# Oldest free page first, stores planned later on the queue, and down groups of 3, 4 and 4 pairs

## The chip, the cores and the metric

The kernel runs as one program on one core of a Trainium2 chip. The metric is the device time of one execution in microseconds (us): 2784.7 us as the median of three runs (2784.27 to 2785.05). The engines are named as the profile names them: PE (TensorE, matmuls), PEld (its weight loads), DVE (VectorE), ACT (ScalarE), POOL (GpSimd) and SP, whose queue issues every DMA of this kernel.

## The reference, cut to what matters

One layer is computed for a prompt of 2048 tokens of width 1024 and for a sample of 32 tokens with a cache of 512. In float32:

```python
mod = einsum(silu(c), w_ada) + b_ada                      # six vectors: shift, scale, gate, twice
h   = rms_norm(x, g_norm1) * (1 + scale1) + shift1
z   = einsum('bld,de->ble', h, w_in)                      # qa ka va | qr kr vr gr
oa  = diff_attention(qa, ka, va, ...)                     # 4 heads, two softmax maps each
orr = rms_unit(retention(rotate(qr), rotate(kr), vr)) * silu(gr)   # 4 heads, a running state
x   = x + gate1 * einsum(concat(oa, orr), w_out)
h2  = rms_norm(x, g_norm2) * (1 + scale2) + shift2
ff  = silu(einsum(h2, w_ff_gate)) * einsum(h2, w_ff_up)   # 2816 columns
x   = x + gate2 * einsum(ff, w_ff_down)
```

Besides both outputs x it returns the normed keys, the values and the last retention state (`k_prompt`, `v_prompt`, `ret_prompt`, and the same for the sample).

## The kernel before, in words

**Stages.** The prompt's 2048 tokens are 16 tiles of 128, in 4 groups of 4. *Start*: the modulation vectors are computed from 16 blocks `wa` of `w_ada`, tiles 0 to 3 of x are normed, and the first input weights are split into two float32r parts (`whi`, `wlo`), which are also stored to `w_scrA`/`w_scrR` and loaded from there by later groups. *Mixer*: for each group, four attention jobs (A0 to A3) and four retention jobs (R0 to R3); a job projects four tiles with three matmuls per product (high x high, high x low, low x high), then does its head. Keys go to `k_prompt` (from tile `qk`), values to `v_prompt` and `v_scr`, transposed keys to `kT_scr`, heads' outputs to `o_scr`. *wout*: the output projection. *gu0* and *gu1*: gate and up projections of the FFN for each half of the tokens. *down0* to *down2*: the down projection.

**Seven products.** From wout on, matrices are multiplied by `quad`: two tiles of rows at a time, as 2x2 blocks with seven products instead of eight. One side is *resident* for the stage (`res`: seven pieces per pair of 128-row blocks), the other is *streamed* (`str`: seven pieces per quad). A piece is a sum of blocks made by DVE, rounded by ACT, and the remainder subtracted by DVE. The down projection has 11 pairs of blocks, which `GROUPS` splits into groups; each group is a stage of 8 quads. A quad of nk pairs is 7 x 3 x nk matmuls of 512 columns: 84 for four pairs, 63 for three. A stage after the first adds the partial y of the stage before from `y_scr`; the last one also multiplies by gate2, adds x (`x2_scr`) and stores `y_prompt`.

**What sets the order.** The code only records operations (`_Plan.add`). `_Plan.schedule` then plays the program through with a cost for each operation (`_cost`, `PACE`) and a latency between engines (`LAT`): each engine takes, of the operations that are ready, the one recorded first (`rank`), if there is room for the tiles that it writes. The order in which an engine took its operations in this play is the order in which they are issued. SP takes DMAs in that order too, and a DMA that has to wait holds all behind it. An operation is ready when the last of its predecessors has ended in the play, plus the latency (`s.at`).

**Pages.** Tiles live in pages of 128 x 1024 floats of SBUF: 27 of kind R (float32r), 16 of kind F, and 7 that are F until the mixer's end and R after it (*swing*); PSUM is 8 banks. `_Places.take` gives a tile the page with the lowest number of those that are free, of the smallest size that fits. A tag's `bufs` bounds how many of its tiles live at once.

Of the kernel before, what the change touches and what calls it, by code (L numbers as in the profile page):

```python
# [12 lines left out]
F32 = mybir.dt.float32  # L13
# [7 lines left out]
P = 128  # L21
# [3 lines left out]
NT = SEQ // P  # L25
# [6 lines left out]
GT = 4  # L32
NG = NT // GT
NEG = -1e30
NR, NFP, NX = 27, 16, 7
GROUPS = ((0, 4), (8, 4), (16, 3))
LAM_INIT = 0.8 - 0.6 * math.exp(-0.3 * 0)
GAMMA = [1.0 - 2.0 ** (-5 - h) for h in range(NH)]


class _Op:
    __slots__ = ("engines", "call", "cost", "preds", "succs", "prio", "rank", "pos", "news", "uses", "left", "at")


class _Engine:
# [12 lines left out]
class _Tile:  # L58


    __slots__ = ("name", "space", "size", "cap", "acc", "old", "order", "block", "left", "dead", "kind", "brief")
# [8 lines left out]
class _View:  # L70


    __slots__ = ("tile", "p0", "np", "off", "dims", "dtype")
# [108 lines left out]
class _Places:  # L182


    def __init__(self, pages, rows, smallest):
        self.rows, self.smallest = rows, smallest
        self.sizes = sorted({rows[i] for i in pages})
        self.free, self.left = {}, 0
        for i in pages:
            self._add(i)  # L190

    def _add(self, i):
        self.free.setdefault(self.rows[i], set()).add((i, 0))
        self.left += 1

# [9 lines left out]
    def take(self, n, keep, but=()):  # L205
        size = self._size(n)
        best = None
        for s in sorted(self.free):
            if s >= size:
                fit = [b for b in self.free[s] if b[0] not in but]  # L210
                if fit:
                    best, (i, off) = s, min(fit)
                    break
        if best is None:
            return None
        whole = best == self.rows[i]
        if whole and self.left <= keep:
            return None
        self.free[best].discard((i, off))
        if whole:  # L220
            self.left -= 1
            if size != best and best > 1024:
                best = 1024
        while best > size:
            best //= 2
            self.free.setdefault(best, set()).add((i, off + best))
        return i, off, size
# [26 lines left out]
class _Plan:  # L254
# [105 lines left out]
    def add(self, engines, name, args, kw):  # L360
        op = _Op()
        op.prio = len(self.ops)
        op.rank = (op.prio + self.bias, op.prio)
        op.engines = engines
        op.call = (name, args, kw)
        op.cost = {e: self._cost(e, name, args, kw) * self.PACE.get(e, 1.0) for e in engines}
        op.preds, op.succs, op.news, op.uses = set(), [], [], set()
        writes = [args[0]] + ([kw["accum_out"]] if kw.get("accum_out") is not None else [])
        reads = list(args[1:]) + [v for k, v in kw.items() if k != "accum_out"]
        for x in reads:  # L370
            r = self._region(x)
            if r is None:
                continue
            t = r[0]
            for o, w, m, a, b in t.acc:
                if w and m & r[1] and a < r[3] and r[2] < b:
                    op.preds.add(o)
            t.acc.append((op, False, *r[1:]))
            op.uses.add(t)
        for x in writes:  # L380
            r = self._region(x)
            if r is None:
                continue
            t = r[0]
            fresh = True
            for o, w, m, a, b in t.acc:
                if m & r[1] and a < r[3] and r[2] < b and o is not op:
                    op.preds.add(o)
                    fresh = False
            if t.old is not None and fresh:  # L390
                self.firsts.append((op, t.old))
            if t.cap is not None:
                op.news.append(t)
            t.acc.append((op, True, *r[1:]))
            op.uses.add(t)
        op.preds.discard(op)
        self.ops.append(op)
        return op
# [15 lines left out]
    def schedule(self, places, swing):  # L414
# [3 lines left out]
        pos = 0.0  # L418
        order = {k: [] for k in places}
        for op in ops:  # L420
            op.pos = pos
            pos += op.cost.get("pe", 0.0)
            op.left = len(op.preds)
            op.at = 0.0
            for p in op.preds:
                p.succs.append(op)
            op.uses = [t for t in op.uses if t.cap is not None]
            for t in op.uses:
                t.left += 1
            for t in op.news:  # L430
                if t.order is None:
                    if t.space == "sb":
                        if any(v.dtype == F32R for o in t.acc for v in self._args(o[0], t)):
                            t.kind = "R"
                    t.brief = max(o[0].prio for o in t.acc) < self.cut
                    t.order = len(order[t.kind])
                    order[t.kind].append(t)
# [41 lines left out]
        while len(started) < len(ops):  # L479
            for e in sorted(idle):  # L480
                skipped, q = [], ready[e]
                while q:
                    pr, op = heapq.heappop(q)
                    if op in started:
                        continue
                    if not room(op):
                        skipped.append((pr, op))
                        continue
                    started[op] = (now, e)
                    idle.discard(e)  # L490
                    end = now + op.cost[e]
                    if e == "pe":
                        turn = op.call[0] == "transpose" and op.call[1][0].dtype == F32R
                        end += 54 * (turned and not turn)
                        turned = turn
                    push(end, 0, e)
                    for s in op.succs:
                        s.at = max(s.at, end + max(self.LAT[e][x] for x in s.engines))
                        s.left -= 1
                        if not s.left:  # L500
                            push(s.at, 1, s)
                    for t in op.uses:
                        t.left -= 1
                        lat = self.LAT[e]["pe"] if t.space == "ps" else max(self.LAT[e].values())
                        t.dead = max(t.dead, end + lat)
                        if not t.left:
                            push(t.dead, 2, t)
                    if op is ops[front]:
                        while front < len(ops) and ops[front] in started:
                            front += 1  # L510
                        while beyond and front < len(ops) and beyond[0][1].pos <= ops[front].pos + self.AHEAD:
                            _, o = heapq.heappop(beyond)
                            for x in o.engines:
                                heapq.heappush(ready[x], (o.rank, o))
                    break
                for x in skipped:
                    heapq.heappush(q, x)
# [67 lines left out]
def kernel(  # L585
# [12 lines left out]
    PE, ANY, AG = _Engine(plan, ["pe"]), _Engine(plan, ["act", "dve"]), _Engine(plan, ["act", "pool"])  # L598
    VG = _Engine(plan, ["dve", "pool"])
    dma = _Engine(plan, ["dma"]).dma_start  # L600

    def open_pool(stack, name, bufs, space=bass.MemoryType.SB):
        pool = stack.enter_context(tc.tile_pool(name=name, bufs=bufs, space=space, reuse_waits="tile"))
# [100 lines left out]
    if True:  # L704
# [99 lines left out]
        def prep_w(out, kind, h, first, sample):  # L804
# [4 lines left out]
            for kp in range(4):  # L809
# [6 lines left out]
                if first:  # L816
                    split(hi, lo, raw)
                    for x, d in zip((hi, lo), kept):
                        dma(d.bitcast(F32), x.bitcast(F32))
                else:  # L820
                    for x, d in zip((hi, lo), kept):
                        dma(x.bitcast(F32), d.bitcast(F32))
# [118 lines left out]
        def attn_back(h, t, vs, g, pt, inv):  # L941
# [8 lines left out]
                    last_u.append(PE.matmul(u[:, :P], lhsT=at[:, b * P:(b + 1) * P], rhs=vs[gv][:, bv, :],  # L950
                                            start=(gg == 0 and b == 0), stop=(gg == g and b == len(blocks) - 1)))
            o = head_out(u[:, :P], inv[:, 0:1], f"{h}_{t}")
            dma(o_scr[t][:, h * P:(h + 1) * P], o)

        def attn_front(h, t, z, kTs, vs):
            g, lt = divmod(t, GT)
            V_t = vs[g]
            A.copy(V_t[:, lt, :], z[:, 256:384])
            qk = qk_norm(z[:, 0:256], f"{h}_{t}")
            dma(k_prompt[t * P:(t + 1) * P, h * P:(h + 1) * P], qk[:, 2:4, :].rearrange("p a b -> p (a b)"))  # L960
            qs = wk.tile([P, 4, 2, 64], F32R, tag="qs", name=f"qs{h}_{t}", bufs=2)
            qh = qs[:, 0:2]
            qd = qk[:, 0:2, None, :].broadcast_to([P, 2, 2, 64])
# [67 lines left out]
        def ret_back(h, t, vr, sg, rk, rT):  # L1031
# [14 lines left out]
            PE.matmul(ra[:, 128:256], lhsT=sc, rhs=vr, start=(S is None), stop=True)  # L1046
            S_cur[h] = S2
            o = ret_out(ra[:, 128:256], sg, name)
            dma(o_scr[t][:, 512 + h * P:512 + (h + 1) * P], o)
            if t == NT - 1:  # L1050
                dma(ret_prompt[h], S2)

# [246 lines left out]
        for n, (g, kind, h) in enumerate(jobs):  # L1299
# [26 lines left out]
            for t in range(g * GT, (g + 1) * GT):  # L1326
# [4 lines left out]
                if kind == "A":  # L1331
                    qT, kb = attn_front(h, t, z, kTs, vs)
                    if t % GT == GT - 1:
                        dma(v_prompt[NG * h + g], vs[g].rearrange("p t c -> p (t c)"))
                        if g < NG - 1:
                            dma(kT_scr[h][g].bitcast(F32), kTs[g].bitcast(F32))
                            dma(v_scr[h][g], vs[g])
                    flush()
                    st_ = attn_mid(h, t, qT, kb, kTs)
                    pend.append(lambda h=h, t=t, vs=vs, st_=st_: attn_back(h, t, vs, *st_))  # L1340
# [475 lines left out]
```

## Time and profile before

| | us |
|---|---|
| median of three runs | 2784.7 |
| the profiled execution | 2783.05 |
| its span, first to last instruction | 2781.3 |
| PE busy | 2685.2 |
| PEld busy | 2229.1 |
| DVE busy | 1896.2 |
| ACT busy | 1307.1 |
| POOL busy | 249.3 |

The mean granted clock of TensorE is 0.984 of 2.4 GHz. PE is idle for 2781.3 - 2685.2 = 96.1 us of the span. Nearly every operation is issued by one line (L580 in the kernel before, L583 after), so groups of instructions are told apart by tiles and by time. In tile names `sb` is a page of SBUF, `ps` a bank of PSUM, `swing` a swing page. `SPq` rows are DMAs being issued: a DMA's row starts when its waits are over, or includes the waits of a merged run of DMAs (x2 and more).

### The profile page before, as it was taken

Reading aid. Unit: us, or ns where it says so; the run is one execution under the profiler, and the core shown is the slowest. Engines: PE = TensorE matmul, PEld = TensorE weight load, DVE = VectorE, ACT = ScalarE, POOL = GpSimd, SP = SyncE. Lnnn points to the kernel's source line nnn. Section 1 sums busy time; section 2 is a strip of 40 time slices with the busy share of each in tenths; the row PEclk is TensorE's granted clock in tenths of the full one; section 3 lists DMA queues with packets and bytes.
Section 4 is the critical chain, followed back from the end, with each engine's and each line's share of the span. In section 5 each row is a group of like instructions: output and inputs, shape, how many; then the busy total and the mean of one; then the engine's idle time right before and its main releaser. Section 6 shows DMA issues by size and latency. Waiting matters only on the chain.

```text
span 2781.3 us, 42347 instructions
## 1 busy us (share of the span) xinstructions
PE 2685.2 (97%) x14606; PEld 2229.1 (80%) x14606; DVE 1896.2 (68%) x4378; ACT 1307.1 (47%) x3241; POOL 249.3 (9%) x474
## 2 busy tenths in 40 slices
PE   6999999999999999989989999998999999999997
PEld 4889888889988888867868888886888887888875
DVE  3776656666676766696785565667655668577799
ACT  4556544666677755555573333243333324242331
POOL 0222111211111111131000000000000000000000
PEclk9999999999999999989999999999999999999999
DMA  7778666644555455546562222324333333355466
GB/s 265 256 270 280 211 207 226 204 153 158 164 170 168 150 189 154 183 139 205 177 202 69 83 61 85 106 83 145 106 99 107 114 121 121 130 180 175 165 229 223
DMA packets 309383, 454.16 MB, mean 163 GB/s; under 512 B 23752, under 2 KB 205196, under 8 KB 309168
## 3 DMA queue, kind: packets, MB, share of 16 engines
q1 hardware_dynamic: 309168, 451.46, 49.6%
q8 instruction: 115, 1.88, 0.3%
q14 instruction: 100, 0.82, 0.1%
HBM read 329.44 MB, written 121.40 MB: 162 GB/s over the span
## 4 chain that ended last, share of the span: by engine, by line
PE 88%; DVE 5%; DMA 3%; ACT 2%; issue 2%; SPq 0%; POOL 0%; DVEq 0%; ACTq 0%; POOLq 0%
PE ps L580 88%; DVE sb L580 4%; ACT sb L580 1%; DMA sb<-in_w_ada 1%; DMA sb<-in_w_ff_down 1%; DMA sb<-w_scrA 0%; SPq L580 0%; DMA sb<-in_w_ff_up 0%; DMA sb<-f_scr 0%; DMA sb<-in_lam_k 0%; DMA sb<-w_scrR 0%; DMA sb<-o_scr 0%; DMA sb<-in_x_prompt 0%; ACT swingTrue L580 0%; DVE swingTrue L580 0%
## 5 line engine op out<-in xcount | busy, mean ns | idle before, releaser
L580 PE MATMUL ps<-sb,sb 128*128 128x512 f32 (+4 forms) x9598 | 1879.1, 368 | 50.2 <-ACT sb L580 16.3
L580 PEld LDWEIGHTS ps<-sb,sb 128*128 128x128 f32 (+1 forms) x9598 | 1437.2, 178 | 323.6 <-issue 43.4
L580 DVE TENSOR_TENSOR sb<-sb,sb 128x512 fp32r<-128x512 f32 (+9 forms) x1305 | 773.3, 626 | 137.8 <-ACT sb L580 111.0
L580 ACT CAST sb<-sb 128x512 fp32r<-128x512 f32 (+5 forms) x726 | 373.9, 543 | 502.3 <-PE ps L580 351.7
L580 PE MATMUL ps<-sb,swingTrue 128*128 128x512 f32 x2124 | 511.8, 391 | 0.4 <-ACT sb L580 0.3
L580 DVE TENSOR_TENSOR sb<-sb,ps 128x512 f32<-128x512 f32 (+3 forms) x460 | 300.8, 658 | 263.4 <-PE ps L580 256.6
L580 PEld LDWEIGHTS ps<-sb,swingTrue 128*128 128x128 f32 x2124 | 396.6, 188 | 87.6 <-issue 2.9
L580 ACT COPY sb<-ps 128x512 f32<-128x512 f32 (+3 forms) x425 | 183.6, 438 | 314.3 <-PE ps L580 281.7
L580 ACT CAST swingTrue<-sb 128x512 fp32r<-128x512 f32 (+1 forms) x231 | 142.1, 622 | 287.8 <-PE ps L580 251.7
L580 ACT ACTIVATE sb<-ps,nm 128x512 f32<-128x512 f32 (+3 forms) x314 | 195.8, 624 | 83.4 <-DVE nm L580 71.2
L580 PE MATMUL ps<-swingTrue,sb 128*128 128x512 f32 x735 | 203.2, 392 | 2.1 <-ACT swingTrue L580 1.2
L580 DVE TENSOR_TENSOR swingTrue<-sb,swingTrue 128x512 fp32r<-128x512 f32 (+1 forms) x231 | 157.2, 684 | 67.6 <-ACT swingTrue L580 67.4
L580 PE MATMUL ps<-ident,sb 128*128 128x128 f32 (+1 forms) x1137 | 176.1, 281 | 19.4 <-DVE sb L580 13.6
L580 PEld LDWEIGHTS ps<-ident,sb 128*128 128x128 f32 (+1 forms) x1137 | 140.2, 144 | 53.1 <-DVE sb L580 18.6
L580 PEld LDWEIGHTS ps<-swingTrue,sb 128*128 128x128 f32 x735 | 138.8, 189 | 32.8 <-ACT swingTrue L580 2.1
L580 DVE TENSOR_REDUCE nm<-ps 128x1 f32<-128x512 f32 (+1 forms) x192 | 128.1, 668 | 30.8 <-PE ps L580 29.9
L580 DVE SCALAR_TENSOR_TENSOR sb<-ps,sb,sb 128x64 f32<-128x64 f32 (+1 forms) x384 | 102.1, 298 | 47.3 <-ACT sb L580 32.9
L580 ACT ACTIVATE sb<-sb 128x512 f32<-128x512 f32 (+5 forms) x180 | 100.8, 563 | 55.4 <-DVE sb L580 36.9
L580 ACT ACTIVATE sb<-ps 128x128 f32<-128x128 f32 (+2 forms) x215 | 74.3, 347 | 94.0 <-PE ps L580 66.5
L580 ACT ACTIVATE sb<-ps,modT,gs 128x128 f32<-128x128 f32 (+1 forms) x248 | 88.9, 471 | 14.6 <-PE ps L580 14.6
L580 DVE TENSOR_TENSOR sb<-sb 128x512 f32<-128x512 f32 (+3 forms) x120 | 71.4, 595 | 33.7 <-DMA sb<-in_w_ff_up 26.2
L580 DVE SCALAR_TENSOR_TENSOR sb<-sb,al 128x512 f32<-128x512 f32 (+2 forms) x141 | 88.6, 678 | 5.9 <-ACT sb L580 5.7
(109 smaller groups left out, 1341.0 us busy)
## 6 DMA issues: line engine op xcount, KB each, us to landing
sb<-w_scrR SPq DMA_DIRECT2D x96, 512.0 KB, 4.9
sb<-w_scrA SPq DMA_DIRECT2D x96, 384.0 KB, 4.7
sb<-in_w_ada SPq DMA_DIRECT2D x48, 512.0 KB, 4.9
sb<-in_w_ff_gate SPq DMA_DIRECT2D x88, 256.0 KB, 5.2
sb<-in_w_ff_up SPq DMA_DIRECT2D x88, 256.0 KB, 3.4
f_scr<-sb SPq DMA_DIRECT2D x88, 256.0 KB, 2.4
sb<-in_w_ff_down SPq DMA_DIRECT2D x44, 512.0 KB, 4.0
sb<-in_x_prompt SPq DMA_DIRECT2D x32, 512.0 KB, 4.3
```

What stands on the lines that cost most here:

```text
L580: inst = getattr(self.eng[e], name)(*[real(x) for x in args], **{k: real(v) for k, v in kw.items()})
```

## The change

Four edits. Pages: `_Places` keeps a running number of when each whole page came free, and `take` picks the page that has been free longest. Stores: a new `put` is a DMA with `slack` 2000 (ns); in the play, whoever waits on its predecessors is ready 2 us later. It is used for the stores of `w_scr`, `k_prompt`, `v_prompt`, `kT_scr`, `v_scr`, and of `o_scr` for tiles 0 to 11; stores of later stages stay as they were. Groups: the down groups have 3, 4 and 4 pairs instead of 4, 4 and 3. Last, `op.uses` is sorted, so that pages that come free at the same moment do so in a fixed sequence.

```diff
-GROUPS = ((0, 4), (8, 4), (16, 3))
+GROUPS = ((0, 3), (6, 4), (14, 4))
@@ class _Places
     def _add(self, i):
+        self.count += 1
+        self.given[i] = self.count
         self.free.setdefault(self.rows[i], set()).add((i, 0))
@@ take
-                    best, (i, off) = s, min(fit)
+                    best, (i, off) = s, min(fit, key=lambda b: (self.given.get(b[0], 0) if s == self.rows[b[0]] else 0, b))
@@ schedule
-            op.uses = [t for t in op.uses if t.cap is not None]
+            op.uses = sorted((t for t in op.uses if t.cap is not None), key=lambda t: (t.name, t.space))
-                        s.at = max(s.at, end + max(self.LAT[e][x] for x in s.engines))
+                        s.at = max(s.at, end + max(self.LAT[e][x] for x in s.engines) + s.slack)
+    def put(out, x):
+        dma(out, x).slack = 2000.0
@@ prep_w
-                        dma(d.bitcast(F32), x.bitcast(F32))
+                        put(d.bitcast(F32), x.bitcast(F32))
@@ attn_back (ret_back alike)
-            dma(o_scr[t][:, h * P:(h + 1) * P], o)
+            (put if t < NT - GT else dma)(o_scr[t][:, h * P:(h + 1) * P], o)
@@ attn_front, and the loop over jobs
-            dma(k_prompt[t * P:(t + 1) * P, h * P:(h + 1) * P], qk[:, 2:4, :].rearrange("p a b -> p (a b)"))
+            put(k_prompt[t * P:(t + 1) * P, h * P:(h + 1) * P], qk[:, 2:4, :].rearrange("p a b -> p (a b)"))
-                        dma(v_prompt[NG * h + g], vs[g].rearrange("p t c -> p (t c)"))
+                        put(v_prompt[NG * h + g], vs[g].rearrange("p t c -> p (t c)"))
...
```

First place, SP's queue in the start stage (the number behind `sb` is the page; w_ada01 blocks are `wa`, in_w_in_a the first raw input weights). Before:

```order
L580 DMA sb31_1577<-in_w_ada01 128x1024
L580 DMA sb28_1574<-in_x_prompt 128x1024
L580 DMA sb29_1575<-in_x_prompt 128x1024
L580 DMA sb30_1576<-in_w_in_a 128x768
L580 DMA sb32_1578<-in_w_ada01 128x1024
L580 DMA sb34_1580<-in_w_ada01 128x1024
L580 DMA sb35_1581<-in_w_ada01 128x1024
L580 DMA w_scrA0_0_0_77<-sb0_1546 128x768
L580 DMA w_scrA0_0_1_78<-sb1_1547 128x768
L580 DMA sb28_1574<-in_w_ada01 128x1024
```

The same stretch of SP's queue now:

```order
L583 DMA sb31_1577<-in_w_ada01 128x1024
L583 DMA sb32_1578<-in_x_prompt 128x1024
L583 DMA sb33_1579<-in_x_prompt 128x1024
L583 DMA sb34_1580<-in_w_in_a 128x768
L583 DMA sb36_1582<-in_w_ada01 128x1024
L583 DMA sb38_1584<-in_w_ada01 128x1024
L583 DMA sb39_1585<-in_w_ada01 128x1024
L583 DMA sb40_1586<-in_w_ada01 128x1024
L583 DMA w_scrA0_0_0_77<-sb0_1546 128x768
L583 DMA w_scrA0_0_1_78<-sb1_1547 128x768
```

The loads of x and of the raw weights go to pages that nothing has used yet instead of pages 28 to 30, which the first `wa` blocks occupy, and the eighth `wa` load stands in front of the first two stores instead of behind them.

Second place, SP's queue at the beginning of the mixer's third group, where the weights of its job R0 are loaded. Before:

```order
L580 DMA out_k_prompt<-sb27_1573 128x128
L580 DMA sb31_1577<-v_scr1_0_250 128x512
L580 DMA o_scr7_150<-sb27_1573 128x128
L580 DMA out_k_prompt<-sb27_1573 128x128 x2
L580 DMA sb1_1547<-w_scrR0_1_1_112 128x1024
L580 DMA sb4_1550<-w_scrR0_1_0_111 128x1024
L580 DMA sb2_1548<-w_scrR0_2_0_113 128x1024
```

Now:

```order
L583 DMA sb29_1575<-v_scr1_0_250 128x512
L583 DMA out_k_prompt<-sb29_1575 128x128
L583 DMA o_scr7_150<-sb27_1573 128x128
L583 DMA out_k_prompt<-sb27_1573 128x128
L583 DMA sb26_1572<-w_scrR0_1_1_112 128x1024
L583 DMA out_k_prompt<-sb27_1573 128x128
L583 DMA sb24_1570<-w_scrR0_1_0_111 128x1024
```

The third `k_prompt` store moves behind the first of the six loads of R0's weights; the other five are still behind it.

Third place, SP's queue as gu1 ends and down0 begins (`f_scr` loads are down0's streamed blocks, `f_scr` stores gu1's last outputs, in_w_ff_down the blocks from which down0's resident pieces are made). Before:

```order
L580 DMA sb33_1579<-f_scr0_1_0_1_186 128x4x128
L580 DMA sb34_1580<-f_scr0_1_0_0_185 128x4x128
L580 DMA f_scr1_1_2_1_202<-sb30_1576 128x512
L580 DMA sb27_1573<-f_scr0_1_0_1_186 128x4x128
L580 DMA f_scr1_0_2_1_196<-sb42_1588 128x512
L580 DMA sb30_1576<-f_scr0_1_0_0_185 128x4x128
L580 DMA f_scr1_0_2_1_196<-sb41_1587 128x512
L580 DMA sb31_1577<-in_w_ff_down 128x1024
L580 DMA sb29_1575<-in_w_ff_down 128x1024
```

Now:

```order
L583 DMA sb36_1582<-in_w_ff_down 128x1024
L583 DMA sb29_1575<-f_scr0_1_0_0_185 128x3x128
L583 DMA sb39_1585<-f_scr0_1_0_1_186 128x3x128
L583 DMA f_scr1_1_2_1_202<-sb40_1586 128x512
L583 DMA f_scr1_0_2_1_196<-sb42_1588 128x512
L583 DMA sb41_1587<-f_scr0_1_0_0_185 128x3x128
L583 DMA sb33_1579<-f_scr0_1_0_1_186 128x3x128
L583 DMA f_scr1_0_2_1_196<-sb38_1584 128x512
L583 DMA sb28_1574<-in_w_ff_down 128x1024
```

The first of the two weight blocks of down0's first pair, which was the eighth DMA of this stretch, stands in front of it; the second one stays at its end.

## Rows read from the trace of the kernel before

**Rows 1.** The page's first part: busy time, share of the span, instructions of each engine

```profile
PE 2685.2 (97%) x14606; PEld 2229.1 (80%) x14606; DVE 1896.2 (68%) x4378; ACT 1307.1 (47%) x3241; POOL 249.3 (9%) x474
```

**Rows 2.** Windows: from:to length, busy of PE, PEld, DVE, ACT, POOL; clock, DMA share, GB/s

```profile
0.00:45.00 45.00, 29.66 (x192) 15.28 (x192) 16.67 (x51) 20.34 (x43) 4.31 (x14) 0.96 0.85 304
540.00:600.00 60.00, 56.25 (x321) 50.49 (x319) 38.45 (x124) 39.79 (x122) 10.83 (x20) 0.94 0.61 200
830.00:900.00 70.00, 65.31 (x462) 57.91 (x461) 44.68 (x131) 50.39 (x147) 11.85 (x25) 0.95 0.56 180
1150.00:1250.00 100.00, 88.01 (x562) 68.76 (x561) 86.22 (x194) 48.85 (x122) 32.34 (x32) 0.90 0.52 158
1405.00:1450.00 45.00, 33.63 (x170) 24.55 (x169) 41.17 (x68) 33.63 (x72) 2.55 (x4) 0.89 0.70 211
1870.00:1900.00 30.00, 18.65 (x103) 12.04 (x102) 26.23 (x44) 13.37 (x23) 0.00 (x0) 0.77 0.77 227
2325.40:2360.00 34.60, 28.30 (x112) 21.64 (x113) 33.21 (x56) 20.36 (x36) 0.00 (x0) 0.95 0.40 138
2480.00:2510.00 30.00, 27.89 (x120) 21.83 (x119) 29.24 (x49) 15.46 (x29) 0.00 (x0) 1.00 0.64 204
2640.00:2660.00 20.00, 17.35 (x68) 13.08 (x67) 18.72 (x32) 11.32 (x21) 0.00 (x0) 0.91 0.63 221
2660.00:2766.60 106.60, 104.70 (x451) 83.51 (x449) 104.19 (x165) 24.61 (x50) 0.00 (x0) 1.00 0.68 232
2766.60:2781.30 14.70, 0.00 (x0) 0.00 (x0) 10.24 (x13) 0.00 (x0) 0.00 (x0) 0.59 0.38 152
```

**Rows 3.** Windows: a stretch of the second down stage

```profile
2550.00:2600.00 50.00, 50.00 (x222) 41.44 (x221) 32.94 (x53) 13.29 (x22) 0.00 (x0) 1.00 0.53 179
```

**Rows 4.** Timeline of SP's queue in the start stage: start, length, operation, count

```profile
2.94 1.84 SPq L580 DMA_DIRECT2D sb<-in_w_ada  x4
7.97 1.52 SPq L580 DMA_DIRECT2D sb<-in_x_prompt  x2
12.01 0.33 SPq L580 DMA_DIRECT2D sb<-in_w_in_a  x1
12.39 1.37 SPq L580 DMA_DIRECT2D sb<-in_w_ada  x3
17.80 1.31 SPq L580 DMA_DIRECT2D w_scrA<-sb  x2
```

**Rows 5.** Windows of 5 us in the start stage

```profile
5.00:10.00 5.00, 3.17 (x21) 0.80 (x21) 1.22 (x6) 0.00 (x0) 0.00 (x0) 1.00 1.02 410
```

**Rows 6.** Timeline of SP's queue as the mixer's third group begins

```profile
557.58 8.13 SPq L580 DMA_DIRECT2D out_k_prompt<-sb  x2
566.60 6.17 SPq L580 DMA_DIRECT2D sb<-w_scrR  x6
```

**Rows 7.** Timeline of PE there: in brackets the idle time before, and what ended it

```profile
576.74 4.84 PE L580 MATMUL ps<-sb,sb 128*128 128x512 f32 x14 [1.78 <-DMA sb<-w_scrR]
```

**Rows 8.** Timeline of PE as down0 begins

```profile
2329.27 11.99 PE L580 MATMUL ps<-sb,sb 128*128 128x512 f32 x44 [3.88 <-ACT sb L580]
```

**Rows 9.** Timeline of ACT as down0 begins

```profile
2328.60 1.34 ACT L580 CAST sb<-sb 128x512 fp32r<-128x512 f32 x2 [3.79 <-DMA sb<-in_w_ff_down]
```

**Rows 10.** Timeline of DVE in down2

```profile
2717.03 8.51 DVE L580 TENSOR_TENSOR sb<-sb,sb 128x1024 f32<-128x1024 f32 x12
...
2747.79 8.51 DVE L580 TENSOR_TENSOR sb<-sb,sb 128x1024 f32<-128x1024 f32 x12
```

**Rows 11.** Groups by form, DVE, 2660 us to the end: count, busy, mean ns

```profile
L580 DVE TENSOR_TENSOR sb<-sb,sb 128x1024 f32<-128x1024 f32 x32 | 38.3, 1217 | 0.0
L580 DVE TENSOR_TENSOR sb<-sb,ps 128x512 f32<-128x512 f32 x48 | 31.1, 680 | 1.2 <-PE ps L580 1.2
L580 DVE TENSOR_TENSOR sb<-sb,sb 128x384 fp32r<-128x384 f32 x43 | 22.8, 551 | 1.0 <-ACT sb L580 1.0
```

**Rows 12.** DMA issues from 2660 us to the end: count, size, median us to landing

```profile
out_y_prompt<-sb SPq DMA_DIRECT2D x16, 512.0 KB, 2.8
```

More of the change, by code (lines that the diff above doesn't have):

```diff
@@ L41 @@
 class _Op:
-    __slots__ = ("engines", "call", "cost", "preds", "succs", "prio", "rank", "pos", "news", "uses", "left", "at")
+    __slots__ = ("engines", "call", "cost", "preds", "succs", "prio", "rank", "pos", "news", "uses", "left", "at", "slack")
 class _Engine:
@@ L187, in __init__ @@
         self.sizes = sorted({rows[i] for i in pages})
-        self.free, self.left = {}, 0
+        self.free, self.left, self.given, self.count = {}, 0, {}, 0
         for i in pages:
@@ L367, in add @@
         op.preds, op.succs, op.news, op.uses = set(), [], [], set()
+        op.slack = 0.0
         writes = [args[0]] + ([kw["accum_out"]] if kw.get("accum_out") is not None else [])
@@ L1048, in ret_back @@
             o = ret_out(ra[:, 128:256], sg, name)
-            dma(o_scr[t][:, 512 + h * P:512 + (h + 1) * P], o)
+            (put if t < NT - GT else dma)(o_scr[t][:, 512 + h * P:512 + (h + 1) * P], o)
             if t == NT - 1:
@@ L1333 @@
                     if t % GT == GT - 1:
-                        dma(v_prompt[NG * h + g], vs[g].rearrange("p t c -> p (t c)"))
+                        put(v_prompt[NG * h + g], vs[g].rearrange("p t c -> p (t c)"))
                         if g < NG - 1:
-                            dma(kT_scr[h][g].bitcast(F32), kTs[g].bitcast(F32))
-                            dma(v_scr[h][g], vs[g])
+                            put(kT_scr[h][g].bitcast(F32), kTs[g].bitcast(F32))
+                            put(v_scr[h][g], vs[g])
                     flush()
```

## The prediction

> **What bounds the kernel now.** I read the page's busy times first. PE is busy for 2685.2 of 2781.3 us [rows 1], so a change of order and pages that leaves every matmul in place can win back at most the 96.1 us in which PE is idle, and what low clock costs around those times. Windows over the span then show where they lie: not spread, but at the borders of stages [rows 2]. PE idles 15.3 us in the first 45; 3.8 and 4.7 us where the mixer's third and fourth groups begin; 12.0 us between mixer and wout; 11.4 at the start of gu0 and 11.4 at gu1; 6.3 as down0 begins. With 6.7 at the later down stages and the 14.7 of the end these are 86 of the 96 us. In each of these stretches from 540 us on the mean clock is 0.77 to 0.95 of 2.4 GHz, so part of them ran at 1.2 GHz. The end is another case: after the last matmul there are 14.7 us, of which DVE works 10.2 [rows 2].
>
> For the down stages idle time understates the loss, so I count matmuls. In full flow a stretch of 50 us holds 222 of them [rows 3], 0.225 us each. The stretch in which down0 begins holds 112 in 34.6 us: 25.2 us of work, 9.4 lost. By the same sum 3.0 us are lost between down0 and down1 (120 in 30.0), 4.7 between down1 and down2 (68 in 20.0), and 5.1 inside down2 (451 in 106.6, where DVE is busy for 104.2) [rows 2]. With the tail that is 36.9 us after gu1.
>
> **The change part by part.** All sums are made against the profiled execution, 2783.05 us with 1.75 around its span; the median of the runs shown lies 1.65 higher, and that is added at the end.
>
> *The tail.* In down2 DVE is the slower engine. The same run of twelve additions and products comes again after 30.76 us, two quads later [rows 10], so a quad takes DVE 15.4 us, while its 63 matmuls take PE 63 x 0.225 = 14.2. DVE falls behind by 1.2 us a quad, and the backlog is what it works off after the last matmul. With four pairs PE has 84 matmuls, 18.9 us. DVE's sums and remainders, 11 a quad, grow from 384 to 512 columns, 0.551 to 0.680 us each [rows 11]: 15.4 + 11 x 0.13 = 16.8. So PE is the slower one, by 2.1 us a quad, and no backlog is left. After the last matmul there then remain one PSUM addition and one of y at 0.68 each and gate, x and the other tile's x at 1.22 each [rows 11], 5.0 us, 0.3 to issue, 2.8 for the store to land [rows 12]: 8.1 instead of 14.7. The sample's four stores, which end the queue before, need only data known long before the end. I take -6.5; bounds -8 (the x addition of the other tile is done earlier) and -3 (half of the backlog stays).
>
> *Inside down2.* Of 5.1 us lost, PE with 2.1 us of slack a quad should win back nearly all: -4, bounds -5 and 0. The extra matmuls are no cost: all three stages together have 1848 before and after.
>
> *Down0 begins.* Now ACT waits 3.79 us for in_w_ff_down and PE 3.88 us behind it [rows 8, 9], and DVE is busy for 33.2 of 34.6 us [rows 2]. Three pairs need 21 resident pieces instead of 28, each one remainder and 4/7 of a sum, 1.07 us of DVE at 0.68 each: 7.5 us less to do before PE runs freely. And the first weight block is asked for seven DMAs earlier; it is enough for the first two products, but the next block is still late. I take -4 of the 9.4; bounds -8 and 0.
>
> *Down1 and down2 begin.* Down1 still needs 28 pieces, but 7 pages more are free in down0: -1 of its 3.0. Down2 now needs 28 instead of 21. That is what down1 needed before, at a loss of 3.0 against 4.7, but 7.5 us of DVE work come on top of a stretch where DVE is busy for 18.7 of 20.0 us [rows 2]. I take 0. Together -1, bounds -2 and +6.
>
> *The start.* SP holds four loads of `wa` out at 4.8 us and then waits until 7.97 for page 28, again until 12.01 for page 30, and until 17.80 for data to store [rows 4], with loads of x and `wa` behind: 9.7 us of waiting in the first 18. The order has free pages for these loads now, and stores behind loads. The cover for this is the DMA engines themselves: they are busy for 0.85 of the first 45 us and move 304 GB/s [rows 2], 13.7 MB. At the 410 GB/s of the best 5 us [rows 5] these would take 33.4 us after the first issue at 2.9, so no more than 8 us can be won; PE's own 29.7 us of work in that stretch and the chains through ACT and DVE hold most of that. I take -3, bounds -8 and +2 (a load that comes one landing later behind the larger burst).
> The Trainium skill's page DMA: Bandwidth & Descriptors, in its section on bandwidth, puts the limit of one core on HBM at about 358 GB/s. By that 13.7 MB need 38.3 us and at most 4 are to be won; the trace's window at 410 speaks against so low a limit, and -3 stands by either.
>
> *The mixer.* As the third group begins, two merged `k_prompt` stores hold SP for 8.1 us; the six loads of R0's weights start behind them, and PE waits 1.78 us for one [rows 6, 7]. The stretch around it costs 3.75 us of idle PE and up to 0.06 x 60 = 3.6 of clock; that of the fourth group 4.7 and 3.5 [rows 2]. Now one of the six loads passes the third store. It is a partial cure: the other five still wait for the third store. Pages in rotation add distance between a tile's last reader and the next writer, in PSUM too. I take -3 of the 15.6; bounds -12 and +7, one such stretch more.
>
> *Wout, gu0, gu1.* 28 pieces resident and few pages free, so that the oldest page is often the only one; PE's order in gu1 is the same instruction for instruction, and no store here is slack. Gu0's last h2 blocks stand earlier, its first weights later. I take -1, bounds -8 and +8.
>
> The sum: -6.5 - 4 - 4 - 1 - 3 - 3 - 1 = -22.5. 2783.05 - 22.5 = 2760.6, and 1.65 more is 2762.2.
>
> **The rivals.** *Only the groups count.* SP waits elsewhere instead, the mixer and the start win nothing: 22.5 - 7 = 15.5, 2769. For it: PE waits for DMA at few places. It is near the forecast, and its reduction to the tail and down2's inside alone (10.5) gives 2774.
>
> *The loss moves to down2's beginning.* 28 pieces have to be made where DVE is nearly full [rows 2], and 7.5 us come back: 2762 + 7.5 = 2770. Against it: while down1 runs, DVE has 17 of 50 us free [rows 3]; but pieces need pages, and these come free with the old ones' last use.
>
> *All border waits in the mixer go.* 15.6 instead of 3: 2762 - 12.6 = 2750. For it: SP's waits are the root of the one that I followed. Against: PE's other idle times there end with ACT and DVE.
>
> *Slower: slack holds pages.* A `k_prompt` or `o_scr` store that is planned 2 us later keeps its tile 2 us longer, and `qk`, `o1` and `ro` have two buffers each. Where heads follow closely, DVE then waits for the buffer, PE for DVE, and the clock falls. One such place costs what the third group's beginning does, 3.75 + 3.6 = 7.35 us [rows 2]. The gain of 22.5 is gone with three of them, of some 30 borders between jobs; with four the time is 2762 + 29.4 = 2792. Against it: the play knows of the held buffers, and puts other work of PE in front.
>
> **How the numbers follow.** What a measurement can tell from no change is about 0.2%, 5.6 us here: 2779.1 to 2790.3 is the same. Forecast 0.5 (its own range 2754 to 2770); only the groups, or the loss moved, 0.25 (2769 to 2777); mixer cured 0.1 (2746 to 2754); the orders of mixer and wout eat up the gain without a single cause 0.08 (within the same); slack holds pages 0.07, mostly slower. So faster 0.84, same 0.1, slower 0.06. The range: the bounds added up reach from -51 to +20, but they will not all fall on one side; 2746 leaves one in ten below, 2780 one in ten above.
>
> **What would show it.** The tail after the last matmul at 8 us, DVE under 0.95 busy in down2, and the stage of down0 beginning with PE waiting less than 2 us show the down part right. In the first 20 us SP should have no wait over 2 us, and PE's idle time in the first 45 falls below 13 us. Four pairs in down2 with DVE still full to the end, or new PE waits over 2 us inside the mixer's jobs, would make the prediction wrong.

## The result, and the profile after

The changed kernel takes 2750.1 us (median; 2747.8 to 2751.6) against 2784.9 (2784.3 to 2787.1) in the same comparison: ratio 0.987, 95% interval 0.9856 to 0.9884, 34.8 us less. The forecast was 2762, its range 2746 to 2780: the direction and the range hold, and 12 us more were won than I summed.

The page's first part, in the columns of [rows 1]:

```profile
PE 2671.7 (97%) x14606; PEld 2222.8 (81%) x14606; DVE 1903.5 (69%) x4382; ACT 1302.1 (47%) x3237; POOL 243.5 (9%) x474
```

The same 14606 matmuls take 13.5 us less of PE's time, and of the span of 2747.8 us PE idles 76.1 instead of 96.1. So 20 of the 33.5 us by which the span shrank are idle time; the rest is the same work in less time. The mean granted clock of the profiled execution is 0.986 instead of 0.984: by an estimate from the two spans (0.016 of 2781.3 against 0.014 of 2747.8 lost) that is about 6 of the 13.5 us. The others were not traced to a place.

Windows of the kernel after, in the columns of [rows 2]; the first four cover the same times, the others the same places:

```profile
0.00:45.00 45.00, 33.68 (x227) 18.68 (x227) 19.09 (x60) 24.25 (x52) 4.19 (x14) 1.00 0.85 328
540.00:600.00 60.00, 58.48 (x349) 52.43 (x348) 43.57 (x143) 43.44 (x130) 11.18 (x21) 0.97 0.51 173
830.00:900.00 70.00, 69.42 (x516) 62.72 (x515) 53.71 (x158) 54.46 (x162) 13.20 (x24) 1.00 0.59 202
1150.00:1250.00 100.00, 87.17 (x495) 68.72 (x497) 86.29 (x177) 45.77 (x110) 27.18 (x30) 0.91 0.40 141
2305.40:2330.00 24.60, 21.61 (x100) 15.10 (x99) 23.33 (x41) 13.63 (x26) 0.00 (x0) 1.00 0.46 153
2580.00:2610.00 30.00, 27.34 (x111) 19.76 (x110) 29.34 (x49) 15.22 (x27) 0.00 (x0) 1.00 0.66 229
2610.00:2738.80 128.80, 128.79 (x569) 106.30 (x567) 116.40 (x165) 28.85 (x48) 0.00 (x0) 1.00 0.59 204
2738.80:2747.80 9.00, 0.00 (x0) 0.00 (x0) 4.88 (x5) 0.00 (x0) 0.00 (x0) 0.78 0.28 117
```

At 0.225 us a matmul, down0 now begins with 2.1 us lost (100 in 24.6), down2 with 5.0 (111 in 30), and inside down2 0.8 are lost (569 in 128.8), with DVE busy for 0.90 of it and PE without a gap. The tail is 9.0.

Places tell little about when time was won, so I split the span at five landmarks that every kernel has: the load of the rope table that opens a group of the mixer (SP), the sample's load of `gate_scr` near the mixer's end (SP), and PE's first run of nine or more narrow matmuls after its wait for `in_w_ff_down` in gu1 (the "gu1 mark"; in e2 and e9 a run of eight stands 1.3 to 1.5 us ahead of it). Lengths in us, one profiled execution each (the experiments are told below):

| kernel | to 1st rope | groups 1 to 3 | 4th rope to gate | gate to gu1 mark | gu1 mark to end |
|---|---|---|---|---|---|
| before | 56.2 | 778.1 | 324.5 | 732.7 | 889.8 |
| after | 49.8 | 769.4 | 315.2 | 740.0 | 873.4 |
| e1 groups only | 55.5 | 779.6 | 324.3 | 737.4 | 877.6 |
| e2 pages only | 52.9 | 771.3 | 324.5 | 734.6 | 887.5 |
| e3 stores only | 57.8 | 769.9 | 313.7 | 735.0 | 891.1 |
| e4 before, nudged | 59.8 | 770.7 | 325.3 | 742.0 | 890.2 |
| e9 k_prompt only | 55.8 | 772.4 | 324.6 | 738.1 | 893.3 |
| e10 w_scr only | 56.1 | 767.2 | 324.0 | 731.8 | 892.6 |
| e11 o_scr only | 57.9 | 773.8 | 313.5 | 733.8 | 892.0 |
| e12 after, slack 6 us | 49.3 | 773.7 | 318.2 | 735.0 | 882.8 |

From before to after: start -6.4, the mixer -18.0 (groups 1 to 3 -8.7, the fourth -9.3), wout and gu0 +7.3, the down stages -16.4. Not every difference is an effect. The instructions of e1 stand in the same order as before's up to the end of gu1, and yet its lengths for groups 1 to 3 and from the gate to the gu1 mark differ by 1.5 and 4.7. The columns in which the kernels fall into two clear sets, with e12 between them, are those of the fourth group (4th rope to gate) and of the down stages (the last). Some profiled executions are also far from their kernel's median: e10's is the fastest of its ten (2773.6, median 2779.7).

SP's queue in the start, after (columns of [rows 4]):

```profile
4.82 0.99 SPq L583 DMA_DIRECT2D sb<-in_x_prompt  x2
5.86 0.45 SPq L583 DMA_DIRECT2D sb<-in_w_in_a  x1
6.35 3.11 SPq L583 DMA_DIRECT2D sb<-in_w_ada  x4
14.89 2.41 SPq L583 DMA_DIRECT2D w_scrA<-sb  x2
```

The holds before x and `wa` at 7.97 and 12.01 [rows 4] are gone: x goes out at 4.82, the second four loads of `wa` at 6.35. What SP still waits for is data to store, until 14.89, of which 4.4 us are put down to ACT; the next loads of x, raw weights and `wa` stand behind these stores. The prediction's sign for this place, no wait of SP over 2 us in the first 20, did not come.

SP and PE where the two `k_prompt` stores held the queue [rows 6], and PE as down0 begins [rows 8], after:

```profile
547.65 0.34 SPq L583 DMA_DIRECT2D out_k_prompt<-sb  x1
548.04 0.89 SPq L583 DMA_DIRECT2D sb<-w_scrR  x1
556.04 0.34 SPq L583 DMA_DIRECT2D out_k_prompt<-sb  x1
556.43 3.13 SPq L583 DMA_DIRECT2D sb<-w_scrR  x5
```

```profile
2313.62 0.50 PE L583 MATMUL ps<-sb,swingTrue 128*128 128x512 f32 x1 [1.51 <-ACT sb L583]
```

One load passes a store; five still wait, behind a store that holds SP for some 7 us, as the order said. PE's wait in down0 fell from 3.88 to 1.51.

### The profile page after: what moved, and what is told of

Its sections match the earlier page's. It is cut to its first block, busy times and chain, and to the rows that moved or that the text cites. A ratio compares the mean times of both kernels' runs of the same rounds, so it can differ in the third digit from the quotient of the medians.

```text
span 2747.8 us, 42176 instructions
## 1 busy us (share of the span) xinstructions
PE 2671.7 (97%) x14606; PEld 2222.8 (81%) x14606; DVE 1903.5 (69%) x4382; ACT 1302.1 (47%) x3237; POOL 243.5 (9%) x474
## 4 chain that ended last, share of the span: by engine, by line
PE 93%; DVE 3%; DMA 2%; ACT 1%; SPq 1%; issue 1%; POOL 0%; ACTq 0%; DVEq 0%; POOLq 0%
PE ps L583 93%; DVE sb L583 2%; ACT sb L583 1%; SPq L583 1%; DMA sb<-in_w_ff_down 1%; DMA sb<-in_x_prompt 0%; DMA sb<-in_w_ada 0%; ACT swingTrue L583 0%; POOL rr L583 0%; DMA sb<-h_scr 0%; DMA sb<-w_scrR 0%; DVE swingTrue L583 0%; DMA sb<-in_t_mask 0%; DMA swingFalse<-in_cache_k 0%; ACT swingFalse L583 0%
## 5 line engine op out<-in xcount | busy, mean ns | idle before, releaser
L583 PE MATMUL ps<-sb,sb 128*128 128x512 f32 (+5 forms) x9737 | 2035.3, 375 | 29.8 <-ACT sb L583 12.7
L583 PEld LDWEIGHTS ps<-sb,sb 128*128 128x128 f32 (+1 forms) x9737 | 1529.6, 179 | 327.0 <-issue 43.7
L583 DVE TENSOR_TENSOR sb<-sb,ps 128x512 f32<-128x512 f32 (+2 forms) x454 | 300.4, 664 | 234.6 <-PE ps L583 231.8
L583 PE MATMUL ps<-swingTrue,sb 128*128 128x512 f32 x1152 | 316.3, 391 | 0.0
L583 PEld LDWEIGHTS ps<-swingTrue,sb 128*128 128x128 f32 x1152 | 217.4, 189 | 46.1 <-ACT swingTrue L583 0.5
L583 PE MATMUL ps<-sb,swingTrue 128*128 128x512 f32 x885 | 226.6, 395 | 7.6 <-ACT swingTrue L583 4.3
L583 PEld LDWEIGHTS ps<-sb,swingTrue 128*128 128x128 f32 x885 | 166.3, 190 | 46.2 <-ACT swingTrue L583 5.4
L583 DVE SCALAR_TENSOR_TENSOR sb<-ps,sb,sb 128x128 f32<-128x128 f32 (+1 forms) x336 | 89.7, 300 | 33.3 <-ACT sb L583 23.7
L583 DVE TENSOR_TENSOR swingTrue<-sb,swingTrue 128x512 fp32r<-128x512 f32 (+1 forms) x125 | 83.7, 674 | 24.3 <-ACT swingTrue L583 24.2
L583 ACT ACTIVATE swingFalse<-ps,nm 128x512 f32<-128x512 f32 (+3 forms) x104 | 66.1, 636 | 29.7 <-DVE nm L583 29.3
```

The lines of the kernel that those rows point to most:

```text
L583: inst = getattr(self.eng[e], name)(*[real(x) for x in args], **{k: real(v) for k, v in kw.items()})
```

## The experiments

The theory after the result: each of the three edits acts by itself, the pages and the stores by freeing SP's queue of holds. The rivals: the groups alone act; or any other plan would have done as well, since the kernel before drew a poor one. e1 to e4 ran together, then e5 to e8, then e9 to e12, each with runs of before (medians 2784.9, 2785.4, 2786.3).

**e1, the groups alone.**

```
-GROUPS = ((0, 4), (8, 4), (16, 3))
+GROUPS = ((0, 3), (6, 4), (14, 4))
```

> The kernel before with the down groups 3, 4, 4 alone. If the down stages' gain is the groups' own (DVE no longer the slower engine in the last stage, fewer resident pieces at the first): 12 to 16 us less than before, and everything up to the end of gu1 within 1 us of before. If part of it came from the page order instead: 6 to 9 us less.

2772.9, ratio 0.9956 (0.9939 to 0.9973): 12.0 less, and 12.2 less from the gu1 mark on. Up to the mark its profile is 5.3 us longer than before's, not within 1 us as expected, though the order is the same.

**e2, the pages alone**, old groups and no slack. This kernel, e3 and e9 to e11 keep the sorting of `op.uses`, which has no run of its own; e9, which has it too, gained nothing.

```
-best, (i, off) = s, min(fit)
+best, (i, off) = s, min(fit, key=lambda b: (self.given.get(b[0], 0) if s == self.rows[b[0]] else 0, b))
```

> The kernel before with the oldest free page first alone (stores without slack, groups 4, 4, 3). Theory A, the mixer's and the start's gain is that loads no longer wait for a page that was just used: 18 to 24 us less at the end of the mixer, the whole run 13 to 20 us less. Theory B, the gain is the stores that no longer hold the queue: the start alone, 5 to 7 us less. Theory C, any other plan would differ as much: between 8 us more and 8 us less.

2774.1, ratio 0.9962 (0.9947 to 0.9977): 10.9 less, in none of the three ranges expected.

**e3, the stores alone**: `put` with its 2000 ns and all its calls, old groups and the lowest free page.

> The kernel before with the slack of stores alone (lowest free page, groups 4, 4, 3). Theory A: 0 to 5 us less. Theory B: 12 to 18 us less, from the beginnings of the mixer's groups. Theory C: between 8 us more and 8 us less.

2769.8, ratio 0.9948 (0.9933 to 0.9962): 15.1 less. The three alone add up to 38.0, together they give 34.8: nearly a sum.

SP's waits in the first 1100 us, in total, number and the longest, of before, e2 and e3:

```profile
SPq L580 <- DVE sb L580: 386.0, 166, 8.0
SPq L580 <- PE ps L580: 203.0, 112, 10.2
```

```profile
SPq L583 <- DVE sb L583: 421.2, 159, 8.6
SPq L583 <- PE ps L583: 110.3, 87, 9.2
```

```profile
SPq L583 <- DVE sb L583: 336.1, 168, 11.4
SPq L583 <- PE ps L583: 315.5, 151, 8.7
```

Each edit does what it says. A wait for PE is mostly a load that needs the page of a tile PE still reads: the oldest page first brings it from 203 to 110 us. A wait for DVE is mostly a store without its data: slack brings it from 386 to 336. But the sum of SP's waits is no price: e3 waits 112.5 us more for PE and 49.9 less for DVE than before, and is the faster. Where a store no longer holds the queue, a load that waits for its page can hold it instead (an example is at e9).

**e4, another plan of the kernel before.**

```
-    PACE = {"pe": 0.95}
+    PACE = {"pe": 0.951}
```

> The kernel before with the planner's factor for matmul costs at 0.951 instead of 0.95, a change that aims at nothing. It shows how much the time moves when the plan merely comes out a little differently. Theories A and B need this to be within 4 us of before; theory C says up to 15 us either way.

2788.0, ratio 1.0012 (1.0003 to 1.0022): 3.1 more. Its groups 1 to 3 are 7.4 shorter than before's, and it loses that elsewhere.

**e5, after with PSUM banks handed out as before** (the lowest free one), the oldest first for SBUF pages only.

```
-(self.given.get(b[0], 0) if s == self.rows[b[0]] else 0, b)
+(self.given.get(b[0], 0) if s == self.rows[b[0]] and self.smallest < 512 else 0, b)
```

> The changed kernel with PSUM banks again by the lowest number; SBUF pages stay oldest first. If the pages' gain is loads that no longer wait for a page just used: within 3 us of the changed kernel. If it is matmuls that no longer wait for a bank to be read out: 6 to 11 us slower than it.

2747.2 (2746.7 to 2750.0), ratio 0.9864 (0.985 to 0.9879): as after. The gain of the pages is SBUF's.

**e6, after with groups of 4, 3 and 4 pairs.**

```
-GROUPS = ((0, 3), (6, 4), (14, 4))
+GROUPS = ((0, 4), (8, 3), (14, 4))
```

> The changed kernel with down groups of 4, 3 and 4 pairs. If the groups' gain comes from the last stage alone, where DVE is no longer the slower engine: within 2 us of the changed kernel. If three pairs in the first stage are worth what the prediction said: 3 to 6 us slower than the changed kernel, lost between gu1 and down0, with the tail still at 9 us.

2759.3 (2752.6 to 2760.0), ratio 0.99 (0.9886 to 0.9915): 9.2 more than after. Down0 begins as before with PE behind ACT for over 3 us:

```profile
2306.40 0.79 PE L583 MATMUL ps<-sb,swingTrue 128*128 128x512 f32 x1 [3.45 <-ACT sb L583]
```

The four pairs last cure the tail in either kernel (9.0 us in both); that three come first is worth 9.2 us more in the median, where 3 to 6 were expected. From the gu1 mark to the end the profiles have 881.5 against 873.4. But e6's profiled execution is the fastest of its four (2752.6; the others took 2759.0 to 2760.0): in the same order as after it reached the mark 5.1 us earlier. The sum of e2 and e3, 26.0 less, would also put the changed kernel with the old groups near 2759, where e6 is, so no median shows that four pairs last win time without three pairs first.

**e7, after with slack on the later stages' stores too** (`h2_scr`, `x2_scr`, `f_scr`, `y_scr`).

```
-            dma(x2_scr[t], x2)
+            put(x2_scr[t], x2)
...
```

> The changed kernel with the slack also on the stores of the later stages (x2_scr, h2_scr, f_scr, y_scr). If a store that is planned too early holds the loads behind it there as well: 4 to 10 us faster, from the borders of gu0, gu1 and down0. If the waits there are for DVE and ACT to make the resident pieces: within 3 us, or slower where slack keeps pages that are scarce.

2748.9 (2747.2 to 2751.2), ratio 0.9869 (0.9854 to 0.9884): no difference from after.

**e8, another plan of the kernel after** (`PACE` 0.951, as in e4).

> The changed kernel with the planner's factor for matmul costs at 0.951 instead of 0.95, aiming at nothing. If the gain is of the rules and not of one lucky plan: within 5 us of the changed kernel, still 28 us or more under the kernel before. If the mixer's part was luck: 8 us or more slower than the changed kernel.

2749.4 (2747.7 to 2750.6), ratio 0.9872 (0.9855 to 0.9888): as after. Two plans on either side, 3.1 and 0.6 apart, while 35 lie between the sides: a lucky plan is not the whole of the gain. A few us of it could still be that.

**e9, e10, e11: which store?** Before with slack on one kind of store each, such as

```
-            dma(k_prompt[t * P:(t + 1) * P, h * P:(h + 1) * P], ...)
+            put(k_prompt[t * P:(t + 1) * P, h * P:(h + 1) * P], ...)
```

> Before with the slack of 2 us on the k_prompt stores alone. Theory 'one place': what slack is worth (15.1 us with all stores) is the hold that the trace showed at the third group's beginning, two merged k_prompt stores; then this alone gives 10 us or more, about 2773. Theory 'many small holds': each kind of store holds SP here and there, and the gain is spread; then this gives a part, 3 to 6 us, about 2780. No change (2785) would say that the k_prompt stores only looked like the cause.

> Before with the slack of 2 us on the stores of the split weights (w_scr) alone; these exist in the first group only, up to about 270 us. 'One place' expects no change, 2785. 'Many small holds' expects 3 to 6 us, about 2780, and all of it visible before the second group begins.

> Before with the slack of 2 us on the o_scr stores alone (all tiles but those of the last group). 'One place' expects no change, 2785. 'Many small holds' expects 3 to 6 us, about 2780. If the three kinds together give about the 15.1 us of all stores, the gain adds up store by store; if each gives nothing, it is their sum that moves the plan.

`k_prompt`: 2788.2, ratio 1.0006 (0.9997 to 1.0016), no gain. `w_scr`: 2779.7, 0.9981 (0.9971 to 0.9991), 6.6 less; its stores lie in the first group, yet of the 10.9 us that its groups 1 to 3 are shorter than before's 7.5 lie in the second and third, against what was expected, and may be luck of the plan or of the execution. `o_scr`: 2772.3, 0.9952 (0.9937 to 0.9967), 14.0 less, nearly all that e3 won. So there is one place that matters most, and it isn't the one I had followed. In e9 the hold of the two `k_prompt` stores did shrink, 2.59 us instead of 8.13 [rows 6], but the queue was not free:

```profile
553.36 2.59 SPq L583 DMA_DIRECT2D out_k_prompt<-sb  x2
564.35 0.33 SPq L583 DMA_DIRECT2D sb<-w_scrR  x1
```

The first load of R0's weights now waits 8.5 us itself, for PE to release its page, and goes out 21.8 us after the third rope load, as in before. So e9 moved the hold from a store to a load and did not take it away. That such a hold need not cost PE anything is shown by e4, which keeps it at 8.15 us:

```profile
559.63 8.15 SPq L580 DMA_DIRECT2D out_k_prompt<-sb  x2
```

There PE has no wait for `w_scrR` (1.78 us in before [rows 7]; 0.68 in e1, in before's order, with a hold of 8.12). The 60 us from the third rope load, of before, e9 and e4:

```profile
544.82:604.82 60.00, 56.25 (x319) 50.28 (x318) 40.23 (x130) 41.96 (x125) 10.08 (x18) 0.94 0.58 192
542.59:602.59 60.00, 58.48 (x357) 52.95 (x356) 42.08 (x139) 45.25 (x137) 10.67 (x20) 1.00 0.60 207
546.89:606.89 60.00, 57.94 (x352) 51.88 (x351) 41.74 (x138) 45.34 (x136) 10.82 (x20) 1.00 0.59 199
```

The place that matters is the beginning of the fourth group. A 70 us window set 4.28 us before the fourth rope load, as [rows 2] have it for before, of e9 and of e11:

```profile
823.90:893.90 70.00, 66.26 (x462) 58.56 (x461) 45.00 (x130) 49.83 (x147) 11.93 (x25) 0.93 0.57 185
```

```profile
827.42:897.42 70.00, 69.22 (x509) 63.09 (x508) 49.87 (x150) 52.91 (x160) 14.79 (x29) 1.00 0.57 192
```

In this window, set so for each of them, before, e1, e2, e4, e9 and e10, in which `o_scr` has no slack, do 462 to 469 matmuls; e3, e11, after and e5 to e8, in which it has 2 us, 507 to 512. No kernel lies between but e12. PE's rows there that carry a wait in brackets, and then SP's longest hold, of before:

```profile
847.59 1.51 PE L580 MATMUL ps<-sb,sb 128*128 128x384 f32 x7 [0.90 <-DMA sb<-w_scrA]
852.32 0.73 PE L580 MATMUL ps<-sb,sb 128*128 128x512 f32 x2 [0.22 <-ACT sb L580]
853.72 1.28 PE L580 MATMUL ps<-sb,sb 128*128 128x384 f32 x4 [0.67 <-ACT sb L580]
856.01 0.51 PE L580 MATMUL ps<-sb 128*128 128x256 f32 x2 [1.00 <-ACT sb L580]
857.87 0.37 PE L580 MATMUL ps<-ident_r,sb 128*128 128x128 f32 x1 [1.20 <-DVE sb L580]
859.54 1.33 PE L580 MATMUL ps<-sb,sb 128*128 128x384 f32 x3 [0.64 <-ACT sb L580]
```

```profile
858.86 15.45 SPq L580 DMA_DIRECT2D sb<-w_scrA  x5
```

The same of e11, with the run of PE ahead of its two waits:

```profile
848.10 5.02 PE L583 MATMUL ps<-sb,sb 128*128 128x512 f32 x28
853.27 0.61 PE L583 MATMUL ps<-sb,sb 128*128 128x384 f32 x2 [0.15 <-ACT sb L583]
854.51 1.66 PE L583 MATMUL ps<-sb,sb 128*128 128x384 f32 x8 [0.62 <-DVE sb L583]
```

```profile
855.33 2.94 SPq L583 DMA_DIRECT2D sb<-w_scrA  x5
```

Before, PE waits 4.6 us in these six rows, mostly for ACT and DVE, and five loads of A's weights hold SP for 15.45 us, most of it after these waits. In e11 a run of 28 products of 512 columns stands there, PE's two waits are 0.8 us, and the hold is 2.94. The slack of a store changed what the planner gives PE. The `o_scr` stores themselves hold SP for up to 4.8 us around here in before, waiting for DVE: the second of these rows starts when that wait is over.

```profile
844.61 0.88 SPq L580 DMA_DIRECT2D sb<-in_w_in_a  x2
850.38 0.33 SPq L580 DMA_DIRECT2D o_scr<-sb  x1
```

In e11 that store holds SP for 2.2 us. The first of the five loads goes out 23.6 us after the fourth rope load instead of 24.6, hardly earlier; the other four follow at once, where in before they wait for PE. Which decision of the planner leads from the slack to PE's fuller order was not followed. The stores of `v_prompt`, `v_scr` and `kT_scr` have no run of their own.

**e12, after with a slack of 6 us.**

```
-        dma(out, x).slack = 2000.0
+        dma(out, x).slack = 6000.0
```

> After with a slack of 6 us in place of 2. If the late data are the trouble and 2 us only just cover them, another 2 to 5 us are won, about 2746. If a held page costs more than a held queue, the rival 'slack holds pages' shows at last and it is slower, 2755 or more. If 2 us already let every load that matters go ahead, it stays within 3 us of 2750.

2756.5 (2756.5 to 2760.8), ratio 0.9898 (0.9883 to 0.9913): 6.5 more than after. Of the 9.3 us won from the fourth rope load to the gate, 3.0 are given back (318.2 against 315.2), and part of it stands in this window:

```profile
818.80:888.80 70.00, 67.61 (x494) 60.60 (x493) 44.61 (x128) 50.83 (x147) 15.31 (x28) 1.00 0.54 180
```

```profile
845.41 9.25 SPq L583 DMA_DIRECT2D sb<-w_scrA  x4
```

494 matmuls instead of 511, and loads of weights hold SP for 9.25 us. More slack is worse, as the rival "slack holds pages" would have it; that held pages are the cause of this is an argument, not shown. Also not settled is why its profiled execution takes 882.8 us after the gu1 mark, where the other kernels with these groups (after, e1, e5, e7, e8) take 873.4 to 878.5; it was the slowest of its four.

## Why the prediction was right, and where it was not

*Groups (-6.5, -4, -4, -1: together -15.5).* The span from the gu1 mark on is 16.4 shorter, with the groups alone 12.2. DVE is no longer the slower engine in down2 (0.90 busy, PE full), as worked out from the quads. The groups of DVE by form from 2610 us to the end:

```profile
L583 DVE TENSOR_TENSOR sb<-sb,sb 128x1024 f32<-128x1024 f32 x32 | 38.6, 1220 | 0.2
L583 DVE TENSOR_TENSOR sb<-sb,ps 128x512 f32<-128x512 f32 x46 | 30.9, 683 | 8.4 <-PE ps L583 8.3
L583 DVE TENSOR_TENSOR sb<-sb,sb 128x512 fp32r<-128x512 f32 x35 | 23.7, 687 | 3.8 <-ACT sb L583 3.6
```

Remainders of 512 columns take 0.687 us, where I had taken 0.680 from [rows 11], and DVE now waits for PE 8.3 us where it had 1.2. *Inside down2* won 4.3 (5.1 to 0.8), *the tail* 5.7 (14.7 to 9.0) for 6.5. In the tail DVE's last work is

```profile
2738.82 0.69 DVE L583 TENSOR_TENSOR sb<-sb,ps 128x512 f32<-128x512 f32 x1
2739.43 4.34 DVE L583 TENSOR_TENSOR sb<-sb,sb 128x1024 f32<-128x1024 f32 x4
```

and ends 5.0 us after the last matmul, as summed; issue and landing then take 4.0, not 3.1. *Down0* won 7.3 of its 9.4 (-4 forecast; the bound was -8), and the loss of 3.0 between down0 and down1 is gone: the two stretches around it hold as many matmuls as full flow, at 0.225 us each.

```profile
2400.00:2430.00 30.00, 30.00 (x134) 24.86 (x133) 24.91 (x41) 18.46 (x35) 0.00 (x0) 1.00 0.49 169
2430.00:2460.00 30.00, 29.92 (x133) 24.44 (x132) 28.86 (x49) 11.21 (x19) 0.00 (x0) 1.00 0.60 209
```

*Down2's beginning* keeps its loss, 5.0 against 4.7: the rival in which the loss moves there did not come. These places add up to 20.0; the span from the gu1 mark on is only 16.4 shorter, and the other 3.6 were lost between the mark and down0.

*The start (-3).* -6.4 to the first rope load, inside the bounds (by the prediction's own sum, 45 - 2.9 - 33.4, the lower one is 8.7 and not 8). Neither edit gives it alone (e2 -3.3, e3 +1.6); the kernels with both have 49.2 to 50.9.

*The mixer (-3; bounds -12 and +7): the step that failed.* It measured -18.0 in one execution of each kernel, beyond the bound. I had followed one hold, of the `k_prompt` stores at the third group, saw that it would be cured in part only, and priced the whole mixer by it. But the hold was not the price: in e4 it stands at 8.15 us and PE does not wait behind it, and in e9, where these stores hold SP for less, a load holds it as long and the time stays as it was. The larger loss that I had in the same rows, the fourth group's beginning (4.7 us idle and 3.5 of clock [rows 2]), I did not follow on the changed order; e11 shows that it is what the slack of the `o_scr` stores cures, some 8 to 11 us from the fourth rope load to the gate in every kernel that has it at 2 us. The other 8.7, in groups 1 to 3, come with the pages (e2 -6.8 there) and with any of the slacks, but the nudged kernel before has as much there; so that part is not proved to belong to the change, though the sum of e2 is. The time of the rival "all border waits in the mixer go", 2750, is what came, yet not its reason: at the fourth group those waits of PE that ended with ACT and DVE went where PE had other work, while the first of the five loads behind SP's holds went out only 1.0 us earlier. That SP's queue had no part in it is not shown.

*Wout, gu0, gu1 (-1; bounds -8 and +8).* +7.3 in the profiles, at the edge of the bounds. Before's execution has one of the shortest lengths there, and e1's, in the same order, has 4.7 more, so at most a part is an effect. e7 shows that later stores are not what is missing there.

That the total fell inside the range is in part luck: the parts add up to -33.5 in the two profiles, where the mixer won 15.0 more than forecast and this part lost 8.3 against its forecast. Of the signs, DVE in down2 (0.90), PE's wait in down0 (1.51) and PE's idle time in the first 45 us (11.3) came, the tail is 9.0 instead of 8, and no new wait of PE over 2 us stands in the mixer; the one on SP's first 20 us failed.

*Only the groups count* (2769 to 2774). The groups alone give 2772.9, but e2 and e3 show that the other two edits count as well. *Slower: slack holds pages.* Not at 2 us; at 6 us 6.5 of the gain go.

The Trainium skill's page Perfetto Trace Analysis says, under DMA Optimizations, that it may make sense, especially with loops or control flow, to give loads to one DMA-capable engine and stores to another. No run here shows what that would do. On the one queue, planning the `o_scr` stores later won 14.0 us (e11), and planning the `k_prompt` stores later won nothing (e9), where a load that waited for its page took over the hold.

## What to carry to other kernels

A hold on an issuing queue has a price only where an engine on the path runs out of work; to price a move of stores, go through each border that shows idle time or a low clock and look at what the new order gives PE there; the length of a hold says nothing yet, and behind a store that is moved away a load can hold the queue as long. Where free buffers of one pool are equal, hand out the one longest free: loads then wait less for a reader that has only just used the page (203 to 110 us of SP's waits here). In a chain of stages that make their own operands, try the smaller group first, so that fewer operands have to be made before the stage runs freely, and the larger last, where the slower helper engine would otherwise leave a tail; here the two together won 12.0 us.

## What the runs showed of the hardware

The same order of instructions gave lengths that differ by up to 5 us over 700 (before and e1 from the gate to the gu1 mark: 732.7 and 737.4), and ten runs of one kernel spread over more than the 0.2% that I had taken as measurable: e10 from 2773.6 to 2784.0, 0.4%. The granted clock was lower in windows with idle PE time, though not in proportion to it. The fourth group's window stood at 0.95 with 4.7 us of idle PE in before, at 0.93 with 3.7 in e9 and at 1.00 with 0.6 in after, so a part of that stretch ran at 1.2 GHz in the first two and none in the last. The first 45 us of after hold 11.3 us of idle PE and stand at 1.00. Nor is every border slow: two of the stretches that the prediction counts, 2480:2510 and 2660:2766.6, stand at 1.00 [rows 2]. A rotation of PSUM banks and always the lowest free one gave the same time (2750.1 and 2747.2).
